# Bias tiles and first projection pieces loaded during the scan, one weight-buffer set, z gated in fours

## The chip, the cores and the metric

The kernel runs as one program on one core of a Trainium2 chip. The metric is the device time of one execution in microseconds (us); the median over several executions is compared between the two versions.

The engines named below: PE (TensorE, matrix multiply), DVE (VectorE), ACT (ScalarE), POOL (GpSimd) and SP (SyncE, which here only issues transfers). SP's transfers stand in one queue, in the order of the program; ACT issues some transfers as well.

## The reference, cut to what matters

One layer of a backbone. 512 latent tokens `x` and 256 context tokens are normalised and projected; three head groups work on the result side by side (a bidirectional state-space scan gated by `silu(z)`, pooling, and neighbourhood attention with a bias table), and one output projection over all 2048 columns joins them:

```python
z, xbc, dtr, pl, q, k, v = project(h, sh1, sc1, norm1_g[i], w_in[i])
ssd_l, _, _ = ssd_mixer(z, xbc, dtr, *ssd_args, st_f, st_b, True)     # ... y * silu(z), rmsnorm
na = neighbourhood_attention(to_heads(q), to_heads(k), to_heads(v), kc, vc, na_rpb[i])
mix = jnp.concatenate([ssd_l, pool_mixer(pl, pool_w[i], pool_scale[i]), na], axis=-1) @ w_out[i]
h = h + g1 * mix
...
h = h + g2 * peer_ffn(u, peer_wq[i], peer_keys[i], peer_u[i], peer_v[i])
return rmsnorm(h, final_g)
```

`peer_ffn` picks 16 of 16384 experts per head and token; it takes the second, longer part of the time and is not touched by the change.

## The kernel before, in words

Every large matmul is made of three: operands are split into a high part (`hi`, written by ACT, line 177) and a low part (`lo`, written by DVE, line 180), and `mm3` (lines 187 to 189) adds high by high, high by low and low by high. Weights come in pieces of 128 x 1024 through a `Stream`: `load` takes a raw buffer (4 KB per partition) and issues the transfer on SP's queue, `split` takes a high and a low buffer (4 KB each). A `Stream` goes round its list of pools in turn.

Buffers come from pools. A pool is a stretch of on-chip memory that is opened and closed; left and right pools grow towards each other. When a pool is closed, its stretch is handed out again as a whole: a tile of a later pool is written only when all users of every closed pool that the later pool overlaps are done.

The stages that matter here:

- **Scan (steps 0 to 60).** The order is written by hand: `at(step, f, ...)` files a call under a step, and the steps run in order; on each engine the instructions run in that order. `ssdin` (right side, opened first, about 42 KB) holds `xsn`, `Bn`, `BT`, `CT`. Beside the scan PE projects z (two halves of 512 columns, four tiles of 128 tokens each) and q. `z_mm` accumulates a z tile in one of four PSUM buffers of `psG`; `z_out` (line 687) applies Silu on ACT into one of two `ztl` buffers and stores it. The scan's own `u_exp` (line 839) uses Exp on ACT. Silu and Exp need different tables, so ACT loads a table whenever it goes from one to the other. At the end `f_gate`, `f_square`, `f_norm`, `f_T`, `f_out` finish the four chunks, and `f_store` (line 915) writes them to `mix_d` in DRAM; the last two stores are at steps 59 and 60.
- **Attention (steps from `A0` = 61).** 32 units (16 pairs `m`, four steps each). For a unit, `a_load` (line 971) brings a bias tile `nb`, `a_scores` (line 986) makes scores on PE into two PSUM buffers, `a_min` (lines 995, 996) adds the bias on DVE, `a_exp` (line 1003) and `a_copy` run on ACT, `a_T` transposes on PE, `a_values` (line 1034) multiplies by the values `vl`, which `v_load` (line 975) brings.
- **Output projection, woven into the attention steps (`O0` = `A0`).** `items` is a list of twelve pieces (pooled rows "p", weights "w", scan rows "s"). `i_load` issues a piece's load, `i_high` puts its high split at the front of step `O0 + OI[i]`, `i_low` does the low split there and loads piece `i + 4`. `o_part` (24 of them, six matmuls each) does the projection with the pieces. The splits of pooled and scan rows go to `mBh`, `mBl`, `mAh`, `mAl` in the pool `o1`, which also holds `h` (the residual, 2 MB, loaded on ACT's queue by line 1180) and `g1r` (line 1091).

At line 1072 a new `Stream` is opened, with four raw and four split buffers of its own ("O", right side, 48 KB); they lie over all of `ssdin`, and `o1` comes after them. The bias tiles lie in `na3`, over the buffers of the projection.

Of the kernel before, what the change touches and what calls it, by code (L numbers as in the profile page):

```python
# [7 lines left out]
F32 = mybir.dt.float32  # L8
# [9 lines left out]
P = 128  # L18
# [19 lines left out]
KVAR = (0, 1, 1, 2)  # L38
# [112 lines left out]
def build(tc, A, out, dbg=None):  # L151
    nc = tc.nc
    V, S, G, PE = nc.vector, nc.scalar, nc.gpsimd, nc.tensor
# [21 lines left out]
    def split(hi, lo, full, eng=None, lows=None):  # L175

        S.activation(hi, full, AF.Copy)  # L177

        def low():
            (eng or V).tensor_tensor(lo, full, hi.bitcast(F32), ALU.subtract)  # L180
        if lows is None:
            low()
        else:
            lows.append(low)

    def mm3(ps, ah, al, bh, bl, start, stop):
        PE.matmul(ps, ah, bh, start=start, stop=False)  # L187
        PE.matmul(ps, ah, bl, start=False, stop=False)  # L188
        PE.matmul(ps, al, bh, start=False, stop=stop)  # L189
# [26 lines left out]
            split(h, l, raw, eng, lows)  # L216
            return h.rearrange("p (k c) -> p k c", k=nk), l.rearrange("p (k c) -> p k c", k=nk)

    def wstream(pools, tag, nraw, nspl, side):
        st = Stream()  # L220
        st.extend(pools, tag, nraw, nspl, side)
        return st.load, st.split

    def kpc(src):
        return src.rearrange("(k p) c -> p k c", p=P)

# [26 lines left out]
    mix_d = tc.dram_tile([16, P, SEQ], F32, name="mix_d")  # L253
# [10 lines left out]
        return r  # L264


    nap = Pools()
    na1 = nap.sb("na1")
    kT = na1.tile([P, 4, NTOK], F32, name="kT")
    qT = na1.tile([P, 4, SEQ], F32, name="qT")  # L270
    vc = na1.tile([P, 2, 512], F32, name="vc")
# [10 lines left out]
    gp = Pools()  # L282
    up = gp.sb("uT")
    uh = up.tile([P, KB, SEQ], F32R, name="uh")
    ul = up.tile([P, KB, SEQ], F32R, name="ul")
    ws = Stream()
    ws.extend(gp, "G", 3, 2, "left")
    wload, wspl = ws.load, ws.split
    gps = Pools()
    psG = gps.ps("psG", bufs=6)  # L290
    psT = gps.ps("psT", bufs=2)
# [45 lines left out]
    a_raw, raws, spls = {}, {}, {}  # L337

    def a_load(n=1):
        for _ in range(n):  # L340
            if a_todo:
                q, kp = a_todo.pop(0)
                raw = slots[(q * 4 + kp) % len(slots)]
                nc.sync.dma_start(raw, A["ada_w1"][q * 4 + kp])
                a_raw[q, kp] = raw.rearrange("p (k s c) -> p k s c", k=2, s=2)
# [13 lines left out]
    def am(q, kp):  # L359
        a_mm(q, kp)  # L360
        a_load()
# [300 lines left out]
    def at(step, f, *a):  # L662
        plan.setdefault(step, []).append((f, a))

    def before(step, f, *a):
        plan.setdefault(step, []).insert(0, (f, a))
# [8 lines left out]
    raws, spls, zacc = {}, {}, {}  # L675
# [40 lines left out]
    def fs(n):  # L716
        return n * FILLED // 48
    for i in range(12):
        at(fs(4 * i), p_load, i + 2)
        at(fs(4 * i + 1), p_split, i + 1)  # L720
        for t in range(4):
            if i < 8:
                at(fs(4 * i + t), z_mm, i // 4, i % 4, t)
                if i % 4 == 3:
                    at(fs(4 * i + t) + 1, z_out, i // 4, t)
            else:
                at(fs(4 * i + t), q_mm, i - 8, t)
        if i >= 8:
            at(fs(4 * i + 3) + 1, q_out, i - 8)
# [32 lines left out]
    st, tmp = {}, {}  # L762
# [25 lines left out]
    def st_plan(i, step, prev, c, w, to, nxt, g):  # L788
        at(step, st_in, i, c, w, g)
        at(step + 1, st_mm, i, prev, c, to, nxt, g)  # L790
        at(step + 2, st_add, i, prev, nxt, g)
# [139 lines left out]
    for c in range(4):  # L931
        b = O1 + OP * c
        for i, (g, d) in enumerate(((0, "f"), (0, "b"), (1, "f"), (1, "b"))):
            at(b + OS[i], o_mm, c, g, d)
            at(b + OS[i] + 1, o_add, c, g, d)
        if c < 3:
            st_plan(10 + c, b + 1, ("f", c), c, enF, toF, ("f", c + 1), 0)
            st_plan(10 + c, b + 4, ("f", c), c, enF, toF, ("f", c + 1), 1)
        f0 = (45, 47, 49, 53)[c]
        at(f0 - 3, f_load, c)  # L940
        at(f0, f_gate, c)
        at(f0 + 1, f_square, c)
        at(f0 + 2, f_norm, c)
        for q4 in range(2):
            at(f0 + 4 + q4, f_T, c, q4)
            at(f0 + 5 + q4, f_out, c, q4)
            at(f0 + 6 + q4, f_store, c, q4)
    assert max(plan) <= FILLED
    for step in range(FILLED + 1):
        run(step)  # L950
# [9 lines left out]
    nat = natp.sb("na3", bufs=4)  # L960
    psS = natp.ps("psS", bufs=2, side="right")
    psP = natp.ps("psP", bufs=1, side="right")
    vls = {}
    units = [(hp, g, hh) for hp in range(4) for g in range(4) for hh in range(2)]
    au, pos_ = {}, {}

    def a_load(n):
        if n < 32:
            hp, g, hh = units[n]
            au[n] = nat.tile([P, 256], F32, name="nb", bufs=4)  # L970
            nc.sync.dma_start(au[n], A["nabias"][hp * 2 + hh, KVAR[g]])

    def v_load(n):
        vls[n] = na2.tile([P, 2, 512], F32, name=f"vl{n}")
        nc.sync.dma_start(vls[n], vw_d[n].rearrange("(f r) c d -> (r c) f d", f=2))
# [64 lines left out]
    A0 = FILLED + 1  # L1040
    for m in range(16):
        a0 = A0 + 4 * m
        for hh in range(2):
            at(max(a0 - 4 + 2 * hh, A0), a_load, 2 * m + hh)
        if m < 4:
            at(a0 + 1, v_load, m)
        at(a0, a_scores, m)
        if m:
            at(a0, a_T, 2 * m - 2)
            at(a0, a_copy, 2 * m - 2)  # L1050
        if m > 1:
            at(a0, a_values, m - 2)
            at(a0 + 1, a_out, m - 2)
        for hh in range(2):
            at(a0 + hh, a_min, 2 * m + hh)
            at(a0 + hh + 1, a_exp, 2 * m + hh)
            at(a0 + hh + 2, a_norm, 2 * m + hh)
        if m:
            at(a0 + 2, a_T, 2 * m - 1)
            at(a0 + 2, a_copy, 2 * m - 1)  # L1060
    a0 = A0 + 64
# [8 lines left out]


    wop = Pools()
    ws = Stream()
    ws.extend(wop, "O", 4, 4, "right")
    wload, wspl = ws.load, ws.split
    op = Pools()
    o1 = op.sb("o1", side="right")
    psO = op.ps("psO", bufs=4)
# [12 lines left out]
            S.activation(dst[:, j * 512:(j + 1) * 512], ps, AF.Copy)  # L1091
    g1r = o1.tile([P, D], F32, name="g1r")

    def w_out(kk, half):
        return kpc(A["w_out"][kk * 256:(kk + 1) * 256, half * 512:(half + 1) * 512])

    def out_mm(acc, w, kk, t, first, last):
        for k2 in range(2):
            k = kk * 2 + k2
            mh, ml, kx = (mAh, mAl, k) if k < 8 else (mBh, mBl, k - 8)  # L1100
            mm3(acc, mh[:, kx, t * P:(t + 1) * P], ml[:, kx, t * P:(t + 1) * P],
                w[0][:, k2, :], w[1][:, k2, :], first and k2 == 0, last and k2 == 1)

    items = [("p", 4), ("w", 4), ("p", 5), ("w", 5), ("s", 0), ("s", 1), ("s", 2), ("s", 3), ("w", 0), ("w", 1), ("w", 2), ("w", 3)]
    raws, spls = {}, {}

    def i_load(i):
        if i < len(items):
            kind, n = items[i]
            raws[i] = wload(w_out(n, 0) if kind == "w" else mix_d[2 * n:2 * n + 2].rearrange("k p t -> p k t") if kind == "p"  # L1110
                            else mix_d[0:8, :, n * P:(n + 1) * P].rearrange("k p t -> p k t"))

    lows = []

    def i_high(i):
        kind, n = items[i]
        raw = raws.pop(i)
        if kind == "w":
            spls[n] = wspl(raw, 2, None, lows)
        elif kind == "p":  # L1120
            ks = slice(2 * n - 8, 2 * n - 6)
            split(mBh[:, ks, :].rearrange("p k t -> p (k t)"), mBl[:, ks, :].rearrange("p k t -> p (k t)"), raw, None, lows)
        else:
            ts_ = slice(n * P, (n + 1) * P)
            split(mAh[:, :, ts_], mAl[:, :, ts_], raw.rearrange("p (k t) -> p k t", k=8), None, lows)
# [3 lines left out]
        i_load(i + 4)  # L1129
    accs = {}  # L1130
    O0 = A0
    OI = [3, 4, 8, 10, 14, 16, 18, 20, 23, 32, 41, 50]
    for i in range(4):
        i_load(i)
    for i in range(12):
        before(O0 + OI[i], i_high, i)
        at(O0 + OI[i], i_low, i)
    at(O0 + 2, row_bc, g1r, lambda: psO.tile([P, 512], F32, name="acc"), 1, 0)

    def o_part(kk, t):  # L1140
        if kk == 4:
            accs[t] = psO.tile([P, 512], F32, name="acc")
        out_mm(accs[t], spls[kk], kk, t, kk == 4, False)
    for j, kk in enumerate((4, 5, 0, 1, 2, 3)):
        for t in range(NX):
            at(O0 + 9 + (4 * j + t) * 59 // 23, o_part, kk, t)
    for step in range(O0, max(plan) + 1):
        run(step)
    assert not plan
# [4 lines left out]
    def out_w(kk, half):  # L1154
        return wspl(wload(w_out(kk, half)), 2)
# [36 lines left out]
    for kk in (6, 7):  # L1192
        w = out_w(kk, 0)
# [4 lines left out]
    accs = [psO.tile([P, 512], F32, name="acc") for _ in range(NX)]  # L1198
    for i, kk in enumerate((4, 5, 0, 1, 2)):
        w = out_w(kk, 1)  # L1200
# [219 lines left out]
    psO = scp.ps("psO2", bufs=3)  # L1420
# [247 lines left out]
    lows = {}  # L1668
# [179 lines left out]
    wop.close()  # L1848
    wxp.close()
    rp.close()  # L1850
    root.close()


# [12 lines left out]
```

## Time and profile before

| | us |
|---|---|
| median of 3 runs | 1878.76 |
| lowest, highest | 1876.68, 1879.7 |
| time of the profiled execution | 1878.0 |
| its span in the profile | 1876.2 |

| engine | busy us | share of the span |
|---|---|---|
| PE | 1806.3 | 96% |
| DVE | 1347.7 | 72% |
| ACT | 852.8 | 45% |
| POOL | 394.3 | 21% |

The chain of work that ended last lies on PE for 88% of the span, on ACT for 4%, on DVE and on transfers for 3% each. So PE is what sets the time, and a change gains where PE stands still or runs at its lower clock. In the picture of 40 slices PE is at nine tenths or more nearly everywhere; one slice, the tenth, shows five tenths, and the scan just ahead of it shows eights.

### The profile page before, as it was taken

The numbers are of one execution on the slowest core, as the hardware profiler recorded it, in microseconds if no ns is written. First come the engines' busy times: TensorE is split into PE (matmuls) and PEld (weight loads), VectorE is DVE, ScalarE is ACT, GpSimd is POOL, SyncE is SP. The second block draws the span as 40 slices with busy tenths as digits, with TensorE's granted clock in tenths as the row PEclk, the third lists the DMA queues.
The fourth block names the chain that finished last, engine by engine and source line by source line (L and its number), as shares of the span: only waits on it lengthen the run. The fifth ranks groups of instructions, "written<-read, shape, count | busy, mean of one in ns | idle before, by whom it ended". The sixth has DMA issues, their size and how long they took to land.

```text
span 1876.2 us, 26317 instructions
## 1 busy us (share of the span) xinstructions
PE 1806.3 (96%) x9703; PEld 1521.2 (81%) x9703; DVE 1347.7 (72%) x2573; ACT 852.8 (45%) x1500; POOL 394.3 (21%) x277
## 2 busy tenths in 40 slices
PE   6999999985999899999999999999999999999997
PEld 4677776653777788999999998888888888888885
DVE  5554127883653558988999896988888878888876
ACT  4332227552653433345767774444444443444434
POOL 1101300151213644430111111211111111111103
PEclk9999999997999999999999999999999999999998
DMA  9545332125532533366899999999999899999971
GB/s 363 169 140 178 109 114 67 37 74 197 164 102 90 163 107 114 116 209 208 308 336 337 347 337 339 401 346 343 357 342 346 336 345 383 347 346 344 358 246 58
DMA packets 190369, 451.46 MB, mean 241 GB/s; under 512 B 13568, under 2 KB 117248, under 8 KB 172288
## 3 DMA queue, kind: packets, MB, share of 16 engines
q1 hardware_dynamic: 150640, 261.61, 41.0%
q0 software_dynamic: 18576, 136.32, 18.9%
q10 hardware_dynamic: 21024, 51.85, 7.4%
q8 instruction: 76, 1.25, 0.3%
q14 instruction: 53, 0.43, 0.1%
HBM read 397.17 MB, written 54.66 MB: 241 GB/s over the span
## 4 chain that ended last, share of the span: by engine, by line
PE 88%; ACT 4%; DVE 3%; DMA 3%; issue 1%; POOL 1%; SPq 0%; ACTq 0%; DVEq 0%; POOLq 0%
PE pu L187 10%; PE pu L189 10%; PE pu L188 10%; PE pv L188 9%; PE pv L189 9%; PE pv L187 9%; PE acc L187 5%; PE acc L189 5%; PE acc L188 5%; PE acc L405 1%; PE acc L407 1%; PE acc L409 1%; PE gdps L1586 1%; PE gdps L1587 1%; PE sps L986 1%
## 5 line engine op out<-in xcount | busy, mean ns | idle before, releaser
L180 DVE TENSOR_TENSOR wl<-wraw,wh 128x1024 fp32r<-128x1024 f32 x290 | 357.0, 1243 | 187.9 <-ACT wh L177 181.7
L177 ACT ACTIVATE wh<-wraw 128x1024 fp32r<-128x1024 f32 x324 | 336.9, 1052 | 227.8 <-PE acc L188 72.1
L187 PE MATMUL pu<-u2h,wh 128*128 128x384 f32 (+2 forms) x1040 | 355.4, 342 | 0.0
L189 PE MATMUL pu<-u2h,wl 128*128 128x384 f32 (+2 forms) x1040 | 350.6, 337 | 1.8 <-DVE wl L180 1.8
L188 PE MATMUL pu<-u2l,wh 128*128 128x384 f32 (+2 forms) x1040 | 350.1, 337 | 0.0
L1525 POOL DMA_INDIRECT row<-in_peer_uv,idxG x128 | 159.5, 1246 | 812.6 <-DVE accG L1539 719.3
L188 PE MATMUL pv<-wl,wwh 128*128 128x512 f32 x768 | 303.4, 395 | 2.1 <-DVE wl L180 2.1
L187 PE MATMUL pv<-wh,wwh 128*128 128x512 f32 x768 | 303.7, 395 | 0.8 <-ACT wh L177 0.8
L189 PE MATMUL pv<-wh,wwl 128*128 128x512 f32 x768 | 303.0, 395 | 0.0
L189 PEld LDWEIGHTS pu<-u2h,wl 128*128 128x128 f32 x1040 | 196.2, 189 | 2.5 <-DVE wl L180 2.5
L188 PEld LDWEIGHTS pu<-u2l,wh 128*128 128x128 f32 x1040 | 196.4, 189 | 1.8
L187 PEld LDWEIGHTS pu<-u2h,wh 128*128 128x128 f32 x1040 | 196.3, 189 | 1.8
L188 PEld LDWEIGHTS pv<-wl,wwh 128*128 128x128 f32 x768 | 144.5, 188 | 35.8 <-DVE wl L180 3.5
L189 PEld LDWEIGHTS pv<-wh,wwl 128*128 128x128 f32 x768 | 144.5, 188 | 34.0
L187 PEld LDWEIGHTS pv<-wh,wwh 128*128 128x128 f32 x768 | 144.5, 188 | 34.1 <-ACT wh L177 1.7
L1539 DVE SCALAR_TENSOR_TENSOR accG<-row,wG,accG 128x1024 f32<-128x1024 f32 x127 | 162.5, 1280 | 4.7 <-ACT wG L1534 3.4
L1530 DVE CUSTOM_DVE_ANT_0 row<-row,u2G 128x1024 f32<-128x1024 f32 x128 | 155.2, 1219 | 0.0
L177 ACT ACTIVATE wwh<-acl 128x384 fp32r<-128x384 f32 x86 | 45.2, 526 | 204.0 <-DVE acl L1698 141.7
L1589 ACT ACTIVATE stg<-gdps 128x512 f32<-128x512 f32 x96 | 101.3, 1168 | 19.4 <-ACT act L1303 10.9
L180 POOL TENSOR_TENSOR wl<-wraw,wh 128x1024 fp32r<-128x1024 f32 x34 | 81.7, 2403 | 112.7 <-ACT wh L177 90.1
L1692 ACT ACTIVATE act<-pu 128x384 f32<-128x384 f32 x42 | 20.6, 490 | 162.8 <-PE pu L189 162.8
L1698 DVE TENSOR_TENSOR act<-act,gd 128x384 f32<-128x384 f32 x42 | 23.5, 558 | 90.1 <-ACT act L1692 90.0
(400 smaller groups left out, 3130.0 us busy)
## 6 DMA issues: line engine op xcount, KB each, us to landing
wraw<-in_peer_ut SPq DMA_DIRECT2D x128, 512.0 KB, 5.9
wraw<-in_peer_uv SPq DMA_DIRECT2D x128, 512.0 KB, 8.8
gd<-gd_d SPq DMA_DIRECT2D x15, 1536.0 KB, 15.7
gd_d<-stg ACTq DMA_DIRECT2D x11, 2048.0 KB, 8.7
wraw<-in_w_in SPq DMA_DIRECT2D x36, 512.0 KB, 5.8
acl<-act_d SPq DMA_DIRECT2D x86, 192.0 KB, 6.0
act_d<-act ACTq DMA_DIRECT2D x84, 192.0 KB, 4.5
kT<-in_ada_w SPq DMA_DIRECT2D x18, 512.0 KB, 4.8
```

Of the source, the lines that this page charges most:

```text
L177: S.activation(hi, full, AF.Copy)
L180: (eng or V).tensor_tensor(lo, full, hi.bitcast(F32), ALU.subtract)
L187: PE.matmul(ps, ah, bh, start=start, stop=False)
L188: PE.matmul(ps, ah, bl, start=False, stop=False)
L189: PE.matmul(ps, al, bh, start=False, stop=stop)
L405: PE.matmul(px, h[:, k, :], uh[:, k, :], start=s, stop=False)
L1525: G.indirect_dma_start(out=rows[k], out_offset=None, in_=A["peer_uv"], in_offset=bass.IndirectOffsetOnAxis(ap=idxG[:, k:k + 1], axis=0))
L1530: V.tensor_tensor_reduce(row[:, 0:D], row[:, 0:D], u2G, 1.0, 0.0, ALU.mult, ALU.add, actG[:, k:k + 1])
L1539: V.scalar_tensor_tensor(accG, row[:, D:2 * D], wG[:, k:k + 1], accG, ALU.mult, ALU.add)
L1589: S.activation(stg[:, :, t0:t0 + 4].rearrange("p a t -> p t a"), ps, AF.Copy, scale=1.0 / GSCALE)
L1692: S.activation(ac[a], pu[:, :TD], AF.Gelu)
L1698: V.tensor_tensor(xq, xq, gds.pop(a), ALU.mult)
```

## The change

- One `Stream` is opened at the start, in a pool `wsp` below everything else on the left: three raw and two split buffers ("G"). It stays to the end. Where "O" was opened with four and four, one raw and two split buffers are added ("O", 20 KB), so that four and four are there again.
- The bias tiles get a pool of their own, `nb`, open from the start. The first four are loaded at steps 57 and 58, the later ones some two steps earlier than before.
- Pieces 0, 1 and 2 of `items` are loaded at steps 56, 57 and 58 and piece 3 at step `O0`; before, pieces 0 to 3 were loaded ahead of step `O0`, behind the opening of "O".
- The first splits move from steps `O0` + 3, 4, 8, 10 to `O0` + 1, 2, 4, 6, the first `o_part` from `O0` + 9 to `O0` + 4; the 24 parts spread over 63 steps in place of 59. The `v_load` of all four groups come within the first seven steps.
- `z_out` of all four tiles of a half is at the step after the last of them, in place of one step after each.

```diff
+    wsp = Pools()
+    ws = Stream()
+    ws.extend(wsp, "G", 3, 2, "left")
+    wload, wspl = ws.load, ws.split
     nap = Pools()
     na1 = nap.sb("na1")
+    nbp = nap.sb("nb", bufs=4)
...
-    ws = Stream()
-    ws.extend(gp, "G", 3, 2, "left")
-    wload, wspl = ws.load, ws.split
...
                 if i % 4 == 3:
-                    at(fs(4 * i + t) + 1, z_out, i // 4, t)
+                    at(fs(4 * i + 3) + 1, z_out, i // 4, t)
...
+    for i in range(3):
+        at(56 + i, i_load, i)
+    for n in range(4):
+        at(57 + n // 2, a_load, n)
...
         for hh in range(2):
-            at(max(a0 - 4 + 2 * hh, A0), a_load, 2 * m + hh)
+            at(a0 + 2 + 2 * hh, a_load, 2 * m + 4 + hh)
         if m < 4:
-            at(a0 + 1, v_load, m)
+            at(A0 + 2 * m, v_load, m)
...
-    ws = Stream()
-    ws.extend(wop, "O", 4, 4, "right")
-    wload, wspl = ws.load, ws.split
+    ws.extend(wop, "O", 1, 2, "right")
...
-    OI = [3, 4, 8, 10, 14, 16, 18, 20, 23, 32, 41, 50]
-    for i in range(4):
-        i_load(i)
+    OI = [1, 2, 4, 6, 14, 16, 18, 20, 23, 32, 41, 50]
+    at(O0, i_load, 3)
...
-    at(O0 + 2, row_bc, g1r, lambda: psO.tile([P, 512], F32, name="acc"), 1, 0)
+    at(O0 + 1, row_bc, g1r, lambda: psO.tile([P, 512], F32, name="acc"), 1, 0)
...
-            at(O0 + 9 + (4 * j + t) * 59 // 23, o_part, kk, t)
+            at(O0 + 4 + (4 * j + t) * 63 // 23, o_part, kk, t)
```

## Rows read from the trace of the kernel before

**Rows 1.** Windows: stretch, length, busy of PE, PEld, DVE, ACT, POOL, clock, DMA.

```profile
440.20:457.70 17.50, 0.01 (x1) 0.00 (x0) 1.38 (x5) 2.05 (x4) 0.00 (x0) 0.59 0.76 276
457.70:470.70 13.00, 11.38 (x45) 7.55 (x46) 7.59 (x18) 8.02 (x17) 3.13 (x2) 0.50 0.50 156
470.70:500.00 29.30, 29.25 (x211) 21.31 (x211) 20.44 (x57) 19.69 (x42) 7.82 (x5) 1.00 0.67 210
```

**Rows 2.** The chain that ended last, 437 to 457: start, length, what.

```profile
437.70 7.67 DMA mix_d<-xsn
445.57 3.70 DMA wraw<-mix_d
...
455.64 1.28 ACT L1003
```

**Rows 3.** Timeline, 429 to 471: start, length, instruction, idle before and releaser.

```profile
429.84 8.23 SPq L915 DMA_DIRECT2D mix_d<-xsn  x4
...
436.72 1.80 ACTq L1180 DMA_DIRECT2D h<-in_x  x4
...
455.01 0.49 DVE L996 CUSTOM_DVE_ANT_0 sps<-sps,nb,mn 128x256 f32<-128x256 f32 x1 [16.19 <-DMA nb<-in_nabias]
...
456.93 0.69 ACT L1003 ACTIVATE pr<-sps,mn 128x512 f32<-128x512 f32 x1
...
457.76 2.74 PE L986 MATMUL sps<-kT,qT 64*128 64x256 f32 x8 [17.55 <-ACT pr L1003]
...
458.27 1.08 ACT L1091 ACTIVATE g1r<-acc 128x512 f32<-128x512 f32 x2
...
459.23 1.07 ACT L177 ACTIVATE mBh<-wraw 128x1024 fp32r<-128x1024 f32 x1
...
462.33 1.22 DVE L180 TENSOR_TENSOR wl<-wraw,wh 128x1024 fp32r<-128x1024 f32 x1
```

**Rows 4.** The chain again: a projection matmul, one pair's scores, transposes, values, upper clock.

```profile
470.95 0.23 PE acc L188
...
473.93 1.06 PE sps L986 x8
474.99 0.59 PE pt L1016 x4
475.58 1.05 PE po L1034 x16
```

**Rows 5.** DMA issues, 425 to 480: size of one, median us to landing.

```profile
h<-in_x ACTq DMA_DIRECT2D x4, 512.0 KB, 4.7
...
mix_d<-xsn SPq DMA_DIRECT2D x4, 256.0 KB, 7.7
mix_d<-y SPq DMA_DIRECT2D x2, 256.0 KB, 2.2
```

**Rows 6.** One window of two us, with PE idle since 440.2.

```profile
442.00:444.00 2.00, 0.00 (x0) 0.00 (x0) 0.00 (x0) 0.00 (x0) 0.00 (x0) 0.84 1.03 398
```

**Rows 7.** Lines 687 and 839, table loads: count, shortest, median, longest ns.

```profile
L687 ACT ACT_TABLE_LOAD  x6: 1283/1283/1283, 309.6 to 387.2; - x6
...
L839 ACT ACT_TABLE_LOAD  x6: 1283/1283/1283, 311.9 to 389.5; - x6
```

**Rows 8.** ACT's timeline at the last z tile of the first half.

```profile
325.09 0.60 ACT L687 ACTIVATE ztl<-acc 128x512 f32<-128x512 f32 x1
325.72 0.33 ACTq L688 DMA_DIRECT2D zs_d<-ztl  x1
326.41 1.28 ACT L839 ACT_TABLE_LOAD   x1 [0.72 <-DVE ms L821]
```

**Rows 9.** DMA issues, 300 to 395: the z stores.

```profile
zs_d<-ztl ACTq DMA_DIRECT2D x8, 256.0 KB, 2.0
```

**Rows 10.** Windows of the scan around the first half's z tiles.

```profile
300.00:326.00 26.00, 26.00 (x110) 17.73 (x109) 22.64 (x36) 19.64 (x39) 2.28 (x1) 1.00 0.22 71
326.00:341.50 15.50, 11.64 (x36) 7.75 (x35) 9.32 (x17) 8.16 (x21) 0.00 (x0) 0.78 0.17 52
```

More of the change, by code (lines that the diff above doesn't have):

```diff
@@ L217, in split @@
             return h.rearrange("p (k c) -> p k c", k=nk), l.rearrange("p (k c) -> p k c", k=nk)
[L219 to L222, printed above, removed]
     def kpc(src):
@@ L947, in build, with w_out, i_load, a_load @@
             at(f0 + 6 + q4, f_store, c, q4)
+    def w_out(kk, half):
+        return kpc(A["w_out"][kk * 256:(kk + 1) * 256, half * 512:(half + 1) * 512])
+    items = [("p", 4), ("w", 4), ("p", 5), ("w", 5), ("s", 0), ("s", 1), ("s", 2), ("s", 3), ("w", 0), ("w", 1), ("w", 2), ("w", 3)]
+    iraws, ispls = {}, {}
+    def i_load(i):
+        if i < len(items):
+            kind, n = items[i]
+            iraws[i] = wload(w_out(n, 0) if kind == "w" else mix_d[2 * n:2 * n + 2].rearrange("k p t -> p k t") if kind == "p"
+                            else mix_d[0:8, :, n * P:(n + 1) * P].rearrange("k p t -> p k t"))
+    units = [(hp, g, hh) for hp in range(4) for g in range(4) for hh in range(2)]
+    au, pos_ = {}, {}
+    def a_load(n):
+        if n < 32:
+            hp, g, hh = units[n]
+            au[n] = nbp.tile([P, 256], F32, name="nb")
+            nc.sync.dma_start(au[n], A["nabias"][hp * 2 + hh, KVAR[g]])
+    for i in range(3):
+        at(56 + i, i_load, i)
+    for n in range(4):
+        at(57 + n // 2, a_load, n)
     assert max(plan) <= FILLED
@@ L963, in build @@
     vls = {}
[L964 to L971, printed above, removed]
     def v_load(n):
@@ L1092, in build @@
     g1r = o1.tile([P, D], F32, name="g1r")
-    def w_out(kk, half):
-        return kpc(A["w_out"][kk * 256:(kk + 1) * 256, half * 512:(half + 1) * 512])
     def out_mm(acc, w, kk, t, first, last):
@@ L1102, in out_mm @@
                 w[0][:, k2, :], w[1][:, k2, :], first and k2 == 0, last and k2 == 1)
[L1104 to L1111, printed above, removed]
     lows = []
@@ L1116, in i_high @@
         kind, n = items[i]
-        raw = raws.pop(i)
+        raw = iraws.pop(i)
         if kind == "w":
-            spls[n] = wspl(raw, 2, None, lows)
+            ispls[n] = wspl(raw, 2, None, lows)
         elif kind == "p":
@@ L1142, in o_part @@
             accs[t] = psO.tile([P, 512], F32, name="acc")
-        out_mm(accs[t], spls[kk], kk, t, kk == 4, False)
+        out_mm(accs[t], ispls[kk], kk, t, kk == 4, False)
     for j, kk in enumerate((4, 5, 0, 1, 2, 3)):
         for t in range(NX):
-            at(O0 + 9 + (4 * j + t) * 59 // 23, o_part, kk, t)
+            at(O0 + 4 + (4 * j + t) * 63 // 23, o_part, kk, t)
     for step in range(O0, max(plan) + 1):
@@ L1850, in build @@
     rp.close()
+    wsp.close()
     root.close()
```

## The prediction

> **What bounds the kernel now.** First the shares: PE is busy for 96% of the span and the chain lies on it for 88%, so only places where PE stands still, or runs at its lower clock, can give time back. The windows by stage show the largest of them at the opening of the attention: PE does nothing for 17.5 us, then works through 13 us at a granted clock of 0.50 (the lower level, 1.2 GHz), and from 470.7 on it is full again at 2.4 GHz (29.25 of 29.3) [rows 1]. The chain says why. The last store of scan rows is issued at 437.70 and lands 7.67 us later; only then is the first piece's load issued (445.57), although the raw buffers of "O" lie over `Bn`, `BT`, `CT`, which nobody reads any more: the stretch of `ssdin` is handed on as a whole, and `xsn` is still being stored [rows 2]. Behind the four pieces in SP's queue come the bias tiles; DVE had waited 16.19 us when it got one at 455.01, then ACT loads its Exp table (1.28) and does the first exponential at 456.93, and PE's next scores start at 457.76 after an idle 17.55, since both score buffers were taken [rows 2, 3]. Meanwhile the 2 MB of `h` were issued at 436.72 and ran ahead of that store, which took 7.7 us to land where stores without such company took 2.2 [rows 3, 5].
>
> How much is lost there? From 440.2 to 470.7 are 30.5 us. PE did in them two pairs of scores, three transposes and one pair of values; at the upper clock that is 2 x 1.06 + 3 x 0.59 + 1.05 = 4.9 us [rows 4]. So 25.6 us of PE are lost, 17.5 by waiting and the rest by the lower clock and by gaps between splits and exponentials.
>
> **The change, part by part.**
>
> *Bias tiles and pieces 0 to 2 early.* They add 7 issues to SP's queue between the store of step 56 and the last two stores. SP issued the last four stores from 429.84 to 438.07, mostly waiting for DVE [rows 3], so issuing costs nothing; without that slack it would be, at the 0.45 us of one `h` issue (1.80 for four), 3 us. The bias tile is then there when the first scores are, and the 16.19 us of DVE go. What is late next? In the new order ACT's first work in the attention is not the exponential but the high split of piece 0 (front of step 62), and it writes `mBh` in `o1`. "O" now takes 20 KB of `ssdin`'s 42, so `o1`, which before lay clear of it, begins inside `ssdin`: all of `o1` waits for the last store of `xsn`, as the raw buffers did [rows 2]. The exponential is queued behind that split, and PE's second scores behind the exponential.
>
> When does that store land? Issued at 437.70 it needs at least 2.2 us (439.9) and at most the 7.67 of before (445.4) [rows 2, 5]. `h` no longer runs beside it, since `h` lies in `o1` too and waits for it. But 2.0 MB of prefetch (three pieces, four bias tiles) are issued ahead of it from about 431.5; at the 398 GB/s of a full window [rows 6] that is 5.0 us, and two other stores share it. I take 441.5, nearer the lower bound, because the prefetch is then about through.
>
> ACT from there: split 1.07, table 1.28, exponential 0.69, `g1r` 1.08, split of piece 1 1.07, second exponential 0.69: 5.9 us, so 447.4 [rows 2, 3]. The old kernel had done the same list at about 461.4 (459.23 and two splits of 1.07 [rows 3]). PE then has the rest of the second scores, two transposes and, new, two projection parts (six matmuls of 0.23 us each [rows 4], 1.4 us), because the splits come at steps 62 to 67 and the parts at 65 and 67. That is 1.06 + 2 x 0.59 + 2 x 1.4 = 5.0 us at the upper clock. PE was idle from 440.2 to 443.4 when its clock fell (0.84 in the window 442 to 444, so 1.00 for its first 1.4 us) [rows 6], and in the new kernel it stands still as long; so some of this work runs at the lower clock, as all of it did until 470.7 [rows 1]. Begun at about 445.5, between the two exponentials, it ends at 450.5 if all runs at the upper clock and at 455.5 if all runs at the lower; I take 454.5, nearer the end that the old kernel showed. Lost: 14.3 - 5.0 = 9.3 us. The gain at the opening is 25.6 - 9.3 = 16.3.
>
> *What is moved into the opening and was covered.* The four `h` issues took 1.80 us on ACT's own queue, in time when ACT was idle [rows 3]; now they become possible at the same moment as the first split. If they come first they cost 1.80, if they fall into a gap nothing; I take 0.9. Piece 3 finds no free raw buffer until piece 0's low split is done (1.07 + 1.22 after 441.5), and its load stands at the head of SP's queue, with later bias tiles and values behind it. It then shares the bandwidth with `h`, where a piece of 512 KB takes about 4.7 us or more [rows 5], and is split at step 67: 0 to 1.5 us of waiting, I take 0.4. The later bias tiles and values are asked for five to eight steps ahead of use, so their delay is covered by PE's work.
>
> *One set of buffers.* The number of raw and split buffers is four and four from the attention on, as before; nothing is added to a load or a split. I cost it at nothing; what it could cost is in the overlap above.
>
> *z in fours.* Each of lines 687 and 839 loads a table six times, 1.283 us each [rows 7]; with one group per half two and two are left, so 8 loads fall away, 10.3 us of ACT. What covers ACT decides what that is worth. In the first half PE is full until 326 (26.00 of 26) and loses 3.9 us plus a lower clock (0.78) in the 15.5 us after [rows 10], when ACT is still between Silu, the table and the scan's Exp [rows 8]. Against the saving stands the pair of `ztl` buffers: the third Silu of a group waits until the first store has landed (2.0 us [rows 9]), about 1 us, and all four release their accumulators only at the group's end, one step before the next half needs them. Counting a group as 1.28 + 4 x (0.60 + 0.33) + 1 + 1.28 = 7.3 us from the last z matmul of the half, which I put at about 320, I reach the next Exp at 327.3; it was at 327.7 (326.41 + 1.28 [rows 8]). In the second half the same sum gives 0.6 us later. So nothing, bounded by 2 us either way.
> The Trainium skill (ScalarE: Activation LUTs, "What ACT_TABLE_LOAD costs") puts a switch at 1283 ns plus a drain of about 1380. The trace agrees on the load and shows no such drain: at 326.41 + 1.28 the next Exp follows at once. By the page's 2.66 us ACT would be spared an estimated 21.3 us instead of 10.3; where PE is full neither shows.
>
> *Sum.* 1878.0 (profiled execution: span 1876.2 and 1.8 around it; 0.8 below the median of the runs) - 16.3 + 0.9 + 0.4 + 0 = 1863.0 us.
>
> **The range of this case.** Store at 445.4: 3.9 less gain; `h` first: 0.9 less; piece 3 late: 1.1 less; z: 2 less. That leaves 7. Store at 439.9: 1.6 more; all of the work at the upper clock: 4 more; `h` issues free and no wait: 1.3 more; z: 2 more. That gives 24. Not all at once: 1856 to 1871.
>
> **Rivals.**
>
> A, larger: the switches spared reach the end as well. The 10.3 us of ACT would have to lie on the path in both halves; for it speaks that ACT is busy 19.64 of the 26 us before 326, against it that PE is full there until 326 [rows 10]. With half of it and the opening's upper end: 1851 to 1856. The skill's rule in "Table sets: the hidden batching unit" (same page), to do all of one set before the next, is this rival.
>
> B, smaller: the last store is no earlier than before, as it now stands behind 2 MB in its own queue, and `h`, started late, takes 2 MB / 398 GB/s = 5.3 us out of the loads of piece 3 and of the first values just when the attention wants them. Gain 16.3 - 3.9 - 5.3 - 2 = 5: 1871 to 1874. For it: 2.2 against 7.7 us [rows 5]. Against: before, the `h` load overtook the store from another queue; the prefetch begins 6 us ahead of it.
> The skill (DMA: Bandwidth & Descriptors, "Queues, rings and completion order") has descriptors of one queue consumed in order, and queues served in turn. That speaks against this change; no row here shows two such orders side by side.
>
> C, not done: the opening is shorter but the attention gives it back, because exponentials, splits and copies, not PE, set its pace once parts come earlier. Against it: PE is at 29.25 of 29.3 us while ACT has 19.69 [rows 1]. Time within 4 us of before.
>
> D, slower: the groups of z hold PE. If a group's stores landed not in 2 but in 8 us, as the `mix_d` store did beside a large load [rows 5], the third and fourth Silu would hold two accumulators for 6 us each, twice, and drop PE's clock: 12 us a half, 24 in all, against 15 gained: 1887. It decides from a landing of about 6 us; nothing large is loaded around 320 or 385, and the eight stores of before landed in 2.0 [rows 9].
>
> **How the numbers follow.** The likeliest case 0.72; A 0.08; B 0.09; C 0.06; D 0.05. What a measurement of this kernel can tell from no change is about 0.2%, 3.8 us. Faster: 0.72 + 0.08 + 0.09 = 0.89; same 0.06; slower 0.05. For 8 in 10 I take the likeliest case and the near parts of A and B: 1854 to 1872.
>
> **What would show it.** Right: DVE's wait for `nb` gone; the first split of `mBh` right behind the landing of the last `mix_d` store, at 440 to 443; first exponential at about 444; PE's idle stretch of 17.5 us down to 5 or less; its clock at 0.50 for less than 12 us; first projection part before 453; four Silu in a row with one table load ahead and one behind, 8 loads fewer; the stages from 700 us on shifted by one amount. Wrong: `mBh` written before that store lands (the gain is larger); ACT waiting for piece 3 or PE for `vl` between 447 and 460 (smaller, B); PE idle around 322 or 388 (D); PE busy below 95% between 460 and 540 (C).

## The result and the profile after

The changed kernel takes 1859.45 us (median of 4 runs, 1858.63 to 1866.38) against 1878.7 (4 runs, 1876.68 to 1879.7): ratio 0.9907, 95% interval 0.9882 to 0.9932 (the ratios in this document are those on record, which can differ by 0.1% from the quotient of the two medians). That is faster by about 1%, 3.6 us below the forecast of 1863.0 and inside its range. The profiled execution is the slowest of the four, 1866.4 us with a span of 1864.6: 11.6 us less than the profiled one of before, where the median fell by 19.3. So the table further down has, beside it, kernels that share its code up to some stage.

The windows of the changed kernel answer to [rows 1]:

```profile
440.20:457.70 17.50, 10.31 (x38) 6.22 (x34) 9.79 (x22) 10.02 (x17) 1.57 (x1) 0.71 0.78 256
457.70:470.70 13.00, 12.29 (x85) 8.62 (x84) 4.34 (x17) 5.40 (x12) 3.13 (x2) 1.00 1.07 346
470.70:500.00 29.30, 26.60 (x174) 19.43 (x174) 18.22 (x51) 17.12 (x36) 7.82 (x5) 0.88 0.42 135
```

The dead 17.5 us now hold 10.3 us of PE, and the 13 us behind them run at 2.4 GHz. But the third row is worse than before: 2.7 us idle and a clock of 0.88, where PE was full. The chain of the changed kernel, against [rows 2], shows both halves of that:

```profile
440.20 4.88 DMA mix_d<-xsn
...
446.37 1.28 ACT L1017
...
454.88 6.79 DMA nb<-in_nabias
...
462.88 8.91 DMA nb<-in_nabias
...
473.40 2.07 PE sps L1000 x6
```

The last store is the first link again, and then the bias tiles, which were to be out of the way, are two links of 6.8 and 8.9 us. The timelines of ACT, DVE and PE say who waited ([rows 3] are those of before):

```profile
445.30 1.06 ACT L177 ACTIVATE mBh<-wraw 128x1024 fp32r<-128x1024 f32 x1 [5.72 <-DMA mix_d<-xsn]
446.37 1.28 ACT L1017 ACT_TABLE_LOAD   x1
447.67 0.69 ACT L1017 ACTIVATE pr<-sps,mn 128x512 f32<-128x512 f32 x1
447.69 0.36 ACTq L1178 DMA_DIRECT2D h<-in_x  x1
```

```profile
467.95 0.49 DVE L1010 CUSTOM_DVE_ANT_0 sps<-sps,nb,mn 128x256 f32<-128x256 f32 x1 [3.49 <-DMA nb<-in_nabias]
471.92 0.49 DVE L1010 CUSTOM_DVE_ANT_0 sps<-sps,nb,mn 128x256 f32<-128x256 f32 x1 [2.95 <-DMA nb<-in_nabias]
```

```profile
448.50 1.22 PE L1000 MATMUL sps<-kT,qT 64*128 64x256 f32 x2 [5.82 <-ACT pr L1017]
451.08 2.07 PE L1000 MATMUL sps<-kT,qT 64*128 64x256 f32 x6 [1.37 <-ACT pr L1017]
473.40 2.07 PE L1000 MATMUL sps<-kT,qT 64*128 64x256 f32 x6 [3.28 <-ACT pr L1017]
```

ACT stands with the split of piece 0 until the last store of `xsn` has landed, and the first exponential and PE's second scores queue behind it, as forecast. Later the waits of DVE for bias tiles that come up to 3.5 us late pass through ACT to PE, which stands still for 3.28 us before 473.40; the clock falls in that wait, and PE starts again at the lower level. In the DMA issues from 425 to 480 the four `h` loads stand in that same stretch, and the bias tiles, a quarter of the size, take as long as they ([rows 5] answer):

```profile
h<-in_x ACTq DMA_DIRECT2D x4, 512.0 KB, 6.1
nb<-in_nabias SPq DMA_DIRECT2D x13, 128.0 KB, 5.6
```

The table loads of lines 684 and 836 are down to two each, against six and six in [rows 7]:

```profile
L684 ACT ACT_TABLE_LOAD  x2: 1283/1283/1283, 320.8 to 385.3; - x2
...
L836 ACT ACT_TABLE_LOAD  x2: 1283/1283/1283, 326.9 to 391.3; - x2
```

**Where the time went, by three stretches.** Three marks stand in every trace: the issue of the last `xsn` store, the first matmul `acc<-u2h,wh` of the stage behind the output projection (in the kernel before at 637.18), and the end of the span. The table gives the first mark (scan), the time from it to the second (opening, attention and projection), and from there to the end (experts), each from one profiled execution. "pv ns" is the mean distance between the starts of neighbouring pv matmuls (128x512, the second product with an expert's weights) that PE runs without a gap (starts less than 0.3 us apart), over 2244 to 2251 of them.

```
kernel          scan    middle  experts   span     pv ns
before         437.70   199.5   1239.1   1876.2   232.6
changed        440.20   193.6   1230.9   1864.6   229.5
z_alone        439.48   198.9   1240.6   1879.0   232.7
z_undone       435.90   192.2   1228.5   1856.6   229.4
bias_alone     438.48   187.7   1238.2   1864.3   232.7
bias_late      439.23   193.8   1228.4   1861.4   229.5
clear_splits   439.15   188.9   1230.7   1858.7   229.5
h_late         436.76   186.6   1228.2   1851.6   229.5
clear_h_late   437.30   183.7   1228.5   1849.5   229.5
old_steps      439.31   187.7   1228.7   1855.7   229.5
set_alone      437.60   199.8   1231.1   1868.6   229.5
swap_before    437.76   199.6   1238.2   1875.6   232.7
rot_after      436.70   192.7   1229.9   1859.3   230.6
two_pools      436.94   202.0   1239.2   1878.2   232.7
```

The change gave 5.9 us in the middle, where 15 were forecast, and 8.2 us in the expert stages, where nothing was; the scan ended 2.5 us later. The rest of this document is about these three numbers. One execution of each is not exact: kernels with the same code in a stretch give 199.5, 199.6 and 202.0 us for the middle (before, swap_before, two_pools), 193.6 and 192.7 (changed, rot_after), and 436.70 to 440.20 for the scan (the six with the changed kernel's scan: it, clear_splits, h_late, clear_h_late, old_steps, rot_after). Differences of the middle under some 2.5 us are not read here.

### The profile page after: what moved, and what is told of

The parts are those of the page before. It is cut to its first block, busy times and chain, and to the rows that moved or that the text cites. A ratio compares the mean times of both kernels' runs of the same rounds, so it can differ in the third digit from the quotient of the medians.

```text
span 1864.6 us, 26316 instructions
## 1 busy us (share of the span) xinstructions
PE 1800.9 (97%) x9703; PEld 1521.1 (82%) x9703; DVE 1347.8 (72%) x2573; ACT 843.5 (45%) x1492; POOL 391.8 (21%) x277
## 4 chain that ended last, share of the span: by engine, by line
PE 88%; ACT 3%; DMA 3%; DVE 3%; issue 1%; POOL 1%; SPq 0%; ACTq 0%; DVEq 0%; POOLq 0%
PE pu L187 10%; PE pu L189 10%; PE pu L188 10%; PE pv L189 9%; PE pv L188 9%; PE pv L187 9%; PE acc L187 5%; PE acc L189 5%; PE acc L188 5%; PE acc L402 2%; PE acc L404 2%; PE acc L406 1%; PE gdps L1584 1%; PE gdps L1585 1%; PE sps L1000 1%
```

## The experiments

**First four: the parts of the change one by one.** The theory was the prediction's: bias tiles and pieces together open the attention, z is worth nothing.

z_alone, the kernel before:

```diff
-                    at(fs(4 * i + t) + 1, z_out, i // 4, t)
+                    at(fs(4 * i + 3) + 1, z_out, i // 4, t)
```

> The kernel before with one edit: z gated four tiles at a time; no piece or bias moved, the weight buffers as before. Theory (z is not on the path that sets the end; what the eight fewer table loads free, 8 x 1.28 us, is ScalarE's idle time): 1876 to 1881 us, within 2 us of before. Rival A (the table loads saved shorten the scan): 1868 to 1874. Rival D (the late stores of each z group hold the scan up): 1881 to 1888, with the last xsn store issued 2 us or more later than in the kernel before (437.7 us).

1878.9 us (11 runs) against 1876.5, ratio 1.0009 (1.0000 to 1.0017): no gain, so rival A's figure falls, and at most 3.2 us lost. The scan ended 1.8 us later. That is the sum of a gain and a loss. What PE loses is here length minus busy time times granted clock, summed over windows of 1 us: from 300 to 380 us it is 9.3 in the kernel before and 7.0 in z_alone, from 380 to 436 it is 6.1 and 10.8. So the first half does win from the spared table loads, as rival A had it, and the second gives it back. PE's timeline there, in the kernel before:

```profile
393.10 0.80 PE L187 MATMUL acc<-uh,wh 128*128 128x512 f32 x1
...
397.50 1.13 PE L864 MATMUL mm<-sfw,CT 128*128 128x512 f32 x2 [0.73 <-ACT ee L839]
```

and in z_alone:

```profile
391.34 0.80 PE L187 MATMUL acc<-uh,wh 128*128 128x512 f32 x1
...
397.61 1.60 PE L864 MATMUL mm<-sfw,CT 128*128 128x512 f32 x2 [2.60 <-ACT ee L839]
398.21 1.42 PE L187 MATMUL acc<-uh,wh 128*128 128x512 f32 x1
399.43 0.63 PE L188 MATMUL acc<-ul,wh 128*128 128x512 f32 x1
```

PE is 1.8 us ahead of the kernel before (391.34 against 393.10), but ACT's `ee`, which it needs next, is not: it starts at 396.95, where it started at 396.85. So PE stands still for 2.60 us in place of 0.73 and its lead is gone. The window behind that has a granted clock of 0.53, so the next matmuls take 0.63 us where they took 0.39, and that is what z_alone pays:

```profile
398.00:400.00 2.00, 2.00 (x5) 1.15 (x4) 1.33 (x4) 0.00 (x0) 0.00 (x0) 0.53 0.00 0
```

It is a small rival D, by another way: the price is 1 to 2 us, and it goes through ACT's turn, not through slow stores (in the changed kernel these land in 2.0 us, as in [rows 9]). The lower clock does not always come. In rot_after, the same code as the changed kernel up to the expert stages, the same wait is followed by the upper clock:

```profile
396.47 1.12 PE L861 MATMUL mm<-sfw,CT 128*128 128x512 f32 x2 [2.60 <-ACT ee L836]
```

and its window:

```profile
398.00:400.00 2.00, 2.00 (x14) 1.73 (x13) 2.00 (x3) 0.00 (x0) 1.53 (x1) 1.00 0.00 0
```

All eight kernels with z in fours have this wait (2.57 to 2.60 us). In five of them the clock fell behind it, and their scans end at 439.15 to 440.20, the changed kernel's among them; in three it did not (rot_after, h_late, clear_h_late), and theirs end at 436.70 to 437.30. The 2.5 us of the scan in the table go with this clock.

z_undone is the changed kernel with that line put back.

> The changed kernel with z gated tile by tile as before. Theory: the 2.5 us by which the scan's last store was issued later after the change (440.20 against 437.70) come from something else than z, so 1857 to 1861 us, no change from the changed kernel's 1859.5. Rival D in small (the second z group's late stores cause those 2.5 us): 1856 to 1858 us, and the last xsn store issued at 438 again. Rival A: 1864 us or more, with 12 table loads for z instead of 4.

1862.3 us (6 runs from 1858.3 to 1867.9), ratio 0.9929 (0.9915 to 0.9943). The scan ended at 435.90, but the median is not lower than the changed kernel's; its runs scatter over 9 us, and 1862.3 lies between the theory's figure and rival A's, so it decides nothing that z_alone leaves open.

bias_alone, the kernel before with `nbp = nap.sb("nb", bufs=4)` and:

```diff
+    for n in range(4):
+        at(57 + n // 2, a_load, n)
...
-            at(max(a0 - 4 + 2 * hh, A0), a_load, 2 * m + hh)
+            at(a0 + 2 + 2 * hh, a_load, 2 * m + 4 + hh)
```

> The kernel before with one edit: the four first bias tiles have a pool of their own and are loaded in the scan, two at each of two late steps; the o_proj pieces stay in the memory that waits for the last store, z is gated as before. Theory (nearly all of the gain is the first pieces' splits and parts that come early enough to fill TensorE while the bias tiles no longer hold VectorE): the bias wait at the opening goes, but the first split is still late, so a part of the 19 us only: 1866 to 1874 us. Rival (the bias wait alone was the opening's price): 1858 to 1863 us, as the whole change. Rival (the bias tiles were hidden behind the pieces anyway): 1876 to 1881.

1866.3 us (6 runs), ratio 0.9947 (0.9931 to 0.9964): a gain of 10 us, inside the theory's figure, but its reason was wrong. The middle fell to 187.7 us, 5.9 less than in the changed kernel, which loads the pieces early as well. ACT's timeline:

```profile
441.54 0.69 ACT L1006 ACTIVATE pr<-sps,mn 128x512 f32<-128x512 f32 x1
...
447.77 1.06 ACT L177 ACTIVATE mBh<-wraw 128x1024 fp32r<-128x1024 f32 x1 [3.81 <-DMA wraw<-mix_d]
```

At the old steps the first exponential stands in front of the first split, and does not wait for the last store: it comes 3.06 us after that store's issue, in the changed kernel 7.47 us after it. No wait of DVE for `nb` is left.

bias_late, the changed kernel with the bias tiles asked for from the attention's first step on:

```diff
-    for n in range(4):
-        at(57 + n // 2, a_load, n)
...
-            at(a0 + 2 + 2 * hh, a_load, 2 * m + 4 + hh)
+            at(max(a0 - 4 + 2 * hh, A0), a_load, 2 * m + hh)
```

> The changed kernel with its bias tiles loaded only from the first step of attention on, as before the change; pieces, weight buffers and z as changed. Theory (the opening needs both): VectorE waits for the first bias tile again, behind the last stores in the queue, until about 450 us; 1863 to 1870 us. Rival (the pieces alone fill the opening, so the bias tiles are hidden): 1857 to 1861 us.

1861.6 us (5 runs), ratio 0.9925 (0.9911 to 0.9939), between the two figures but nearer the rival's; the middle is 193.8 us, within 0.2 us of the changed kernel's. So the rival is right in the main: as long as ACT's first work is a split that waits for the store, a bias tile that comes 3.7 us late is hidden behind it. The two edits of the opening don't add. Bias tiles alone gave 11.8 us of the middle; with the early splits there, loading them early gives nothing that these executions show.

**Next four: what holds the middle of the changed kernel up.** Suspects were the wait of the first split, the company of `h`, and the early steps.

clear_splits, the changed kernel with `h` and `g1r` in a pool that takes the stretch over `xsn`, so that the splits' tiles lie clear of it:

```diff
+    o0 = op.sb("o0", side="right")
+    o0.tile([P, 400], F32, name="gap")
+    h = o0.tile([P, NX, D], F32, name="h")
+    g1r = o0.tile([P, D], F32, name="g1r")
```

> The changed kernel with the first h and g1r tiles in a pool of their own that takes the memory over the scan's last mix_d tiles, so that the first splits' tiles lie clear of it. Theory (the first split waits for the landing of the last xsn store, 4.9 us after its issue, through the memory that it is handed): the first mBh split stands at 438 to 442 us instead of 445.3, ahead of the store's landing, and the time falls by 3 to 5 us, to 1854 to 1857. Rival (the first split waits for piece 0, or the end of attention's opening is set by the bias tiles that come late at 455 to 472): the split is earlier and the time stays within 2 us of 1859.5.

h_late, the changed kernel with the loads of `h` put into the attention:

```diff
+    for t in range(NX):
+        at(O0 + 24 + 8 * t, nc.scalar.dma_start, h[:, t, :], A["x"][t * P:(t + 1) * P, :])
```

> The changed kernel with the four 128-row loads of h issued by ScalarE within attention, 24, 32, 40 and 48 steps behind the first split, instead of at its opening. Theory (h's loads, the pieces and the bias tiles crowd the queues from 447 to 470 us, and h is needed by none of it): VectorE's waits for bias tiles at 455 to 472 shrink to under 2 us each and the time falls by 2 to 5 us, to 1855 to 1858. Rival (the bias tiles are late because they stand behind the pieces in SyncE's own queue): the waits stay, and so does the time, 1858 to 1861 us.

clear_h_late has both.

> Both of the edits before this one together: the first splits' tiles clear of the scan's memory, and h loaded late. Theory: their gains add, 1850 to 1855 us. Rival (the one's gain is taken by the other's wait, the bias tiles): 1855 to 1859 us.

old_steps, the changed kernel with `OI = [3, 4, 8, 10, ...]` and the first parts at `O0 + 9 + (4 * j + t) * 59 // 23`, as before.

> The changed kernel with the steps of the splits and of the first o_parts as before the change (splits at 3, 4, 8 and 10, parts from 9 on, counted from the opening) while piece loads and bias tiles stay early. Theory (the early steps give TensorE the parts by which it gets through the opening; without them scores alone fill it, which wait for the exp chain): 2 to 5 us of the gain are lost, 1861 to 1865 us. Rival (the gain is the bias tiles' and the stores' alone): 1858 to 1861 us.

Against 1876.5 us of before (9 runs): clear_splits 1858.7, ratio 0.9908 (0.9893 to 0.9923); h_late 1855.9, 0.9902 (0.9885 to 0.9919); both 1851.8, 0.9874 (0.9859 to 0.9890); old_steps 1858.3, 0.9908 (0.9893 to 0.9923). By the time alone only the two together stand apart from the changed kernel (0.9907, 0.9882 to 0.9932), and narrowly: the intervals still overlap a little. The traces part them all. ACT's timeline of clear_splits:

```profile
438.42 1.05 ACT L177 ACTIVATE mBh<-wraw 128x1024 fp32r<-128x1024 f32 x1
...
442.20 0.69 ACT L1017 ACTIVATE pr<-sps,mn 128x512 f32<-128x512 f32 x1
443.93 0.60 ACT L1106 ACTIVATE g1r<-acc 128x512 f32<-128x512 f32 x1 [0.96 <-DMA mix_d<-xsn]
```

The first split stands before the last store is even issued (439.15), and what waits for its landing is `g1r`, which holds ACT up for 0.96 us: the wait of the first split was the memory's, as the prediction and this run's theory had it. The first exponential comes 5.5 us earlier than in the changed kernel, and the middle is 4.7 us shorter. But the time stays at the rival's figure, and DVE still waits for bias tiles:

```profile
467.32 0.49 DVE L1010 CUSTOM_DVE_ANT_0 sps<-sps,nb,mn 128x256 f32<-128x256 f32 x1 [4.30 <-DMA nb<-in_nabias]
```

In h_late no such wait is left, though SP's queue holds the pieces ahead of the bias tiles as before: so the order in the queue alone does not make them late, the 2 MB of `h` beside it do. The Trainium skill (DMA: Bandwidth & Descriptors, "Queues, rings and completion order") has each DMA engine serve its queues in turn; the changed kernel's trace fits that, as a bias tile of 128 KB took 5.6 us, about as long as a load of 512 KB from the other queue (6.1), but pieces stood ahead of the tiles too, and no row parts the two. The middle of h_late is 7.0 us shorter than the changed kernel's; both edits together make it 9.8 shorter, of 11.7 if they added in full. One window from 440 to 475 us in four kernels, first that of before:

```profile
440.00:475.00 35.00, 15.89 (x70) 10.64 (x70) 11.86 (x31) 12.82 (x24) 4.29 (x3) 0.61 0.68 232
```

The changed kernel:

```profile
440.00:475.00 35.00, 24.40 (x130) 16.18 (x126) 16.84 (x45) 17.63 (x33) 5.30 (x4) 0.81 0.81 262
```

h_late:

```profile
440.00:475.00 35.00, 28.95 (x178) 20.76 (x179) 21.77 (x54) 23.18 (x45) 7.83 (x5) 0.85 0.68 213
```

clear_h_late:

```profile
440.00:475.00 35.00, 30.10 (x190) 21.99 (x191) 23.80 (x62) 23.35 (x48) 7.82 (x5) 0.90 0.76 234
```

PE does 70, 130, 178 and 190 matmuls there. Part of the step from 130 to 178 is the scan, which ended some 3 us earlier in the last two kernels; the middles above are free of that. old_steps also misses its theory and meets its rival's figure: the early steps were to be worth 2 to 5 us, and without them the middle is 5.9 us *shorter*, with the first exponential ahead of the first split:

```profile
442.36 0.69 ACT L1017 ACTIVATE pr<-sps,mn 128x512 f32<-128x512 f32 x1
...
445.63 1.06 ACT L177 ACTIVATE mBh<-wraw 128x1024 fp32r<-128x1024 f32 x1
```

Its middle, 187.7 us, is also that of bias_alone, which loads no piece early. So beside early bias tiles the early pieces add nothing that these executions show, and the changed kernel falls short of bias_alone by what the new steps of the splits cost. The old steps together with `h` loaded late were not run.

**Last four: the expert stages.** In every kernel with the one set of weight buffers they last 1228 to 1231 us, in those without it 1238 to 1241.

set_alone, the kernel before with nothing but the buffers changed:

```diff
+    wsp = Pools()
+    ws = Stream()
+    ws.extend(wsp, "G", 3, 2, "left")
+    wload, wspl = ws.load, ws.split
...
-    ws = Stream()
-    ws.extend(wop, "O", 4, 4, "right")
-    wload, wspl = ws.load, ws.split
+    ws.extend(wop, "O", 1, 2, "right")
```

> The kernel before with one edit: one set of weight buffers kept from the gate stage to the end, in place of a new set opened for the output projection; pieces, biases and z are loaded, split and stepped as before. Theory, new (in the changed kernel and in every variant of it with the one set, TensorE runs the expert stages after 620 us some 8 to 9 us shorter than before, with the mean interval between the 128x512 pv matmuls 229.5 ns against 232.7; the variant with early biases alone and the old buffers has none of that): 1867 to 1870 us, with the opening as long as before, pv intervals of 229.5, and all of the gain behind 620 us. Rival, the prediction's (one set is worth 0; the expert stages gain from the earlier opening): 1875 to 1879 us, pv intervals of 232.7.

1869.4 us (6 runs) against 1875.8, ratio 0.9966 (0.9953 to 0.9979); in the profiled execution the middle is that of before (199.8 us) and the experts take 7.9 us less. The theory holds: this edit alone is 0.34% of the time. Its mark is seen in a stretch of pv matmuls without any wait, in the timeline of before (first and last of 20):

```profile
1314.43 0.40 PE L187 MATMUL pv<-wh,wwh 128*128 128x512 f32 x1
...
1318.84 0.39 PE L188 MATMUL pv<-wl,wwh 128*128 128x512 f32 x1
```

and of set_alone (again 20):

```profile
1318.69 0.39 PE L189 MATMUL pv<-wh,wwl 128*128 128x512 f32 x1
...
1322.99 0.39 PE L187 MATMUL pv<-wh,wwh 128*128 128x512 f32 x1
```

19 distances in 4.41 us are 232 ns each, in 4.30 us 226 ns. Over all of them the means are 232.6 and 229.5 ns; 2304 pv matmuls times 3.1 ns are 7.1 us. Neither stretch has a wait; on the mean each matmul follows the one ahead of it a little sooner.

Three more runs asked what of the buffers it is. swap_before, the kernel before with the pools `ex` and `gl` opened in the other order, moves the pv weights `wwh` and `wwl` by 12288 bytes:

```diff
+    gl0 = Pools()
+    gl = gl0.sb("gl", bufs=4)
     esp = Pools()
     ex = esp.sb("ex", bufs=2)
     glp = Pools()
-    gl = glp.sb("gl", bufs=4)
```

> The kernel before with the pools ex and gl opened in the other order, so that the tiles wwh, wwl and act of the expert stage lie 12288 bytes a partition higher; nothing else is moved. Theory (the place in memory of wwh and wwl, the operands that are loaded as weights in the pv matmuls, sets their interval; the one set of buffers moved them by 28672 bytes): the pv interval changes from 232.7 ns, by up to 3.2 ns on 2304 matmuls, so up to 7 us: 1869 to 1874 us. Rival (it is the turn in which the weight buffers come, or another tile's place): 232.7 ns again and 1875 to 1879 us.

1876.4 us, ratio 1.0002 (0.9993 to 1.0011), 232.7 ns: the rival. The place of `wwh` and `wwl`, moved by this much, is not it.

rot_after is the changed kernel with `ws.j += 1` ahead of the expert stages.

> The changed kernel with the counter of split buffers set on by one where the expert stages begin, so that the halves of an expert's weights use the four buffers in another turn; every tile keeps its place. Theory (the turn of the buffers decides how TensorE's matmuls follow one another): pv intervals go from 229.5 ns back towards 232.7 and the time to 1863 to 1867 us. Rival (the place of the tiles in memory does): intervals of 229.5 ns and 1857 to 1861 us.

1863.8 us (4 runs), ratio 0.9937 (0.9923 to 0.9952), and 230.6 ns, between the two: with every tile in its place the turn of the buffers moves the interval by 1.1 of the 3.1 ns, so neither theory is the whole. The expert stages of this execution (1229.9 us) are not longer than the changed kernel's (1230.9), and the intervals of the two ratios overlap, so the 1.1 ns is seen in the interval alone.

two_pools, the kernel before with its set grouped as in the changed one, in the same 48 KB:

```diff
-    ws.extend(wop, "O", 4, 4, "right")
+    ws.extend(wop, "O", 3, 2, "right")
+    ws.extend(wop, "P", 1, 2, "right")
```

> The kernel before with one edit: its set of weight buffers for the output projection and the experts, four raw and four split buffers, is made of two pools (three raw and two split, one raw and two split) in the same 48 KB, as the one set of the changed kernel is; nothing is moved in time and no other tile changes its place. Theory A (the gain behind 620 us comes from how the four split buffers are grouped: in pools of two the high and the low part of a weight lie 8192 bytes a partition apart, in a pool of four 16384): pv intervals of 229.5 ns or near, 1867 to 1871 us. Theory B (it comes from where the buffers or the tiles u2h and u2l lie, 28672 bytes a partition from their place before): pv intervals of 232.7 ns and 1874 to 1879 us.

1879.7 us (11 runs) against 1877.2, ratio 1.0013 (1.0004 to 1.0022), 232.7 ns: the grouping by itself is not it. One thing differs from the changed kernel beside the place: there the counter of split buffers has run through 33 splits before the output projection, an odd number, and here it starts at 0, so the buffers of the two pools are taken in other pairs. rot_after, with 34, has the pairs of two_pools; between these two the place makes 2.1 ns (230.6 against 232.7), and the turn makes the other 1.1. So most of it is theory B, the place, by exclusion: in the changed kernel three raw and two split buffers lie at the other end of the memory, and `u2h`, `u2l` and the expert tiles 28672 bytes further on. Which of these tiles it is, and by what in the chip, stays open; moving `u2h` and `u2l` alone was not tried, nor two pools in the old place with the changed kernel's turn.

## Why the prediction was right, and where it was not

The number was right by two errors of opposite sign, which is luck: the opening gave less than forecast, and the expert stages, where nothing was forecast, made up for it.

- *25.6 us lost at the opening:* right. Length minus busy time times granted clock, summed over 1 us windows from 436 to 475, gives 25.0 for the kernel before.
- *The landing of the last store, 441.5:* at the late end of its bounds (439.9 to 445.4). It landed 4.88 us after its issue where 3.8 was taken, and the issue itself came 2.50 us later, which the prediction had not counted (the clock behind the wait in the scan, see z_alone): the split stands at 445.30. In rot_after, the same code up to there but with the upper clock in the scan, issue and split are at 436.70 and 441.44.
- *ACT's list of 5.9 us:* right; from 445.30 to the end of the second exponential, 450.94, are 5.6.
- *9.3 us lost in the changed opening:* right until 456 (10.0 by the same sum). The step that failed comes after it: "The later bias tiles and values are asked for five to eight steps ahead of use, so their delay is covered by PE's work." Two of the tiles took 6.8 and 8.9 us to land beside `h`, DVE waited 0.32, 3.49 and 2.95 us for three in a row, and by the same sum PE lost another 4.2 us from 456 to 475, so 14.2 in all: a gain of 10.8 where 16.3 were forecast. Behind it 1.1 more than before were lost until 590 and 2.4 more from 590 to 640, which leaves 7.3; 5.9 are what the whole middle gained by its two marks. The 1.4 between them are PE's own work, which counts 166.9 us at the upper clock between the marks in place of 165.5; why is not shown.
- *Rival B* was the right mechanism with the wrong victim. `h` did take bandwidth from what the attention wants, h_late shows 6 to 7 us of it (against rot_after and the changed kernel); but piece 3 kept no one waiting, the bias tiles did. Its other half, the store behind the prefetch, is 1.1 us.
- *The queue on ACT* was seen (the exponential behind the split), but its alternative was not priced: at the old steps, with the exponential first, the middle is 5.9 us shorter (old_steps). The splits' new steps are a loss, and no run shows the early pieces earning it back: bias_alone, which has neither, has the same 187.7 us as old_steps.
- *`h` issues, 0.9:* hidden; they stand behind exponentials (447.69). What `h` cost was its traffic.
- *One set of buffers, 0:* wrong. It was argued from the number of buffers and the waits alone; alone it gave 6.4 us by the medians (1875.8 to 1869.4) and 7.9 in the trace.
- *z, nothing within 2 us:* about right in size (z_alone: 0 to 3.2 us lost), but as the difference of two effects: 2.3 us won in the first half, as in rival A, and 4.7 lost in the second, as in rival D but through ACT's turn and the clock behind it. Four loads instead of twelve, as forecast.
- *C:* its sign, PE below 95% from 460 to 540, was just missed (76.2 of 80 us). What is lost there lies before 500 (PE at 26.6 of 29.3 us from 470.7 on) and comes from the bias tiles; from 500 to 590 PE is busy for 89.6 of 90 us.
- *The signs:* the wait for the first `nb` gone, the split right behind the store's landing and eight table loads fewer came as named. The first exponential (447.67, named 444), PE's idle stretch (5.82 us, named 5 or less), the lower clock (some 17 us up to 479, named under 12) and the first projection part (453.85, named before 453) came late or long, and the stages from 700 us on were not shifted by one amount but became shorter.

Of the forecast gain of 15.0 us the middle gave 5.9, the scan took 2.5 more, and the buffers gave 8.2 that nobody asked for: 11.6 in the profiled execution. In rot_after the same sum is 1.0 + 6.8 + 9.1 = 16.9, nearer to the 19.3 of the medians. The best kernel here is clear_h_late, 1851.8 us: it gets from the opening the 15 us that were forecast for it (199.5 to 183.7 are 15.8).

## What to carry to other kernels

When a wait is taken away at the head of a stage, write down for each in-order engine what its first instruction will be: here an early split that needed the stage's last store went ahead of an exponential that did not need it, and ate half of what the early bias tiles had won. Loads that nobody needs for 100 us (`h` is first used at 558) belong behind those that are needed now, even on another queue. And a change of buffers is not free of effect because their number stays: time it alone.

## What the runs showed of the hardware

Matmuls of one shape, at the upper clock and with no wait, follow one another at intervals that depend on the buffers: the mean of some 2250 pv matmuls was 232.6 to 232.7 ns in all five kernels with the old set, 229.4 to 229.5 in all eight with the one set in its own turn, and 230.6 with its turn shifted by one. Within a group the means differ by less than 0.1 ns. Pairs with a gap between them are left out, and the clock is the upper one but for one short stretch in three of the fourteen. The Trainium skill (TensorE: Matmul & The Clock Gate, "Wait — 56ns, not 53.3ns?") gives 215.7 ns for 512 columns at that clock; here, with a weight load for every matmul, all three are 6 to 8% above that, and the measurement decides.

A wait of PE can be dearer than its length, and the same wait is not always equally dear: 2.60 us of standing still were followed by a granted clock of 0.53 in z_alone and of 1.00 in rot_after, and the scans with the one outcome and the other ended some 2 to 3 us apart.
